# A hybrid mixer and mixture of experts on one core: GLA's decays in another PSUM bank and later, four scalings on VectorE, a longer warm-up, and part of the last expert pair's preparation one pair earlier

## The chip, the cores and the metric

The kernel runs on one core of one Trainium2 chip. The metric is the device time of one execution in microseconds (us); lower is better. PE is TensorE, DVE is VectorE, ACT is ScalarE, POOL is GpSimd, SP is SyncE, whose queue carries the weights.

## What is computed

One layer on 256 tokens of 1024 channels, all float32. A layer norm; one input projection whose columns feed an RWKV-7 group (8 heads of 64) and a GLA group (4 heads, key 64, value 128); the output projection; a residual layer norm; a top-4-of-32 mixture of experts (MoE) with a clamped SwiGLU; and a last residual layer norm. What matters here:

```python
def rwkv7_mixer(...):
    ...
    a = sigmoid(a0 + ad @ a_up)
    kk = k * k_k
    kk = kk / maximum(sqrt(sum(kk * kk, -1)), 1e-12)
    k = k * (1.0 + (a - 1.0) * k_a)
    y = rwkv7_recurrence(r, decay, k, v, kk, a)
    ...
    y = y + sum(r * k * r_k, -1) * v          # the bonus
def gla_chunked(q, k, v, gk):
    b = cumsum(gk, axis=3)                    # inside chunks of 64
    q_e = q * exp(b) * (DK ** -0.5)
    k_e = k * exp(-b)
    ...
def moe_ffn(x, ...):
    top_val, top_idx = top_k(x @ router_w + router_b, 4)
    gate = softmax(top_val)
    # for each expert e: the tokens that chose it
    h = x[tok] @ w1[e] + b1[e]
    gt = minimum(h[:, :D_FF], 7.0); up = clip(h[:, D_FF:], -7.0, 7.0)
    act = (up + 1.0) * gt * sigmoid(1.702 * gt)
    y = y.at[tok].add((act @ w2[e] + b2[e]) * gate)
x = layer_norm(x + mix); x = layer_norm(ALPHA * x + y)
```

## The kernel before

The code is written for a framework that tracks tiles and their buffers; its scheduler decides the order of the instructions on each engine from the order of the code, from priorities, and from `tc.issue_after(x)`, which keeps what is inside it behind instruction x. PSUM has eight banks of 128x512 float32: in the mixer the names p, r, s and a have two each, in the MoE g has four, x two and o two. A new `bank("p")` waits until the one before the last of that name has been read.

**The mixer, 0 to some 230 us.** The input projection is done with float32r, a shorter format that PE takes in one pass where float32 takes two (two rows of the trace for one matmul). Each weight block is cut by `split` into a high part (ACT, L382) and a low part (DVE, L385); a block of 128x512 then feeds twelve matmuls of 128x256 (L395, L396 and L397). `shift` (ACT L423, DVE L424) reads a finished projection bank and so frees it. Between the projections stand small steps of the recurrence: sums of squares (L526), a reciprocal root on ACT and DVE (its ACT part is L239), its transposes (L532) and copy (ACT, L533), its spreading over heads (L548), the scalings of k by `a` (L554, four of 128x256, on ACT), the bonus (L575), and GLA's cumulated decays (L608, four matmuls of 128x128) with their two exponentials on ACT (L610 and L611). Then come the scores of the two halves of the sequence (`scores`, L623, masked on DVE at L626), two triangular inverses on DVE (their last line is L667), the recurrence by chunks, the output projection (L992) with its norm (L994), and the router.

**The MoE, to the end.** The experts go in 16 pairs, e2 = 0 to 15, with 64 places for each expert. `places` (DVE) makes a 0/1 choice `so` of the tokens; PE gathers the chosen rows with it (L1286, from `xres`), and ACT and DVE scale the result into `xg` (L1105, L1106). For each expert of the pair W1 is applied (L1307: 8 steps of k, four matmuls each, four weight slots of 2 MB), a bias added (L1317), `swiglu` done (DVE L1084, L1086 to L1088, ACT L1085) and its result transposed (L1096). W2 follows (L1382, two slots for each expert); its result is scaled by the gate into a high and a low part (`oc`, ACT L1390, DVE L1391), and spread to the tokens by float32r matmuls with the transposed choice `soT` (L1257) in the next pair's W1, and added to `y` (L1262).

The last pair differs. Its choice times gate, `sg`, is transposed into a float32 `sgT` (L1331), and the rows of the last norm's weights are spread to all partitions (`row`, L1223, copied at L1340 into `xres`) in the middle of its W1. Its W2 goes in nine pieces of columns (L1416): each is copied by ACT into `oq` (L1418), spread by float32 matmuls (L1421), added to `y` by DVE (L1423), and, for the second expert, taken into the norm's statistics (L1425). The last norm and the stores follow.

The weights come in a list in the order of use: `fetch` issues them on SP's queue (L281), 2 MB each, into ten slots, as slots come free. Four of the list are W_out, then each pair has eight W1 slots and four W2 slots; the last pair's W2 comes in smaller pieces (`w2l`).

Of the kernel before, what the change touches and what calls it, by code (L numbers as in the profile page):

```python
# [10 lines left out]
F32 = mybir.dt.float32  # L11
# [4 lines left out]
OP = mybir.AluOpType  # L16
# [123 lines left out]
def mix_moe(ctx: ExitStack, tc: tile.TileContext, A, out, dbg=None):  # L140
# [18 lines left out]
    def bank(tag):  # L159
        return psum[0].tile([128, 512], F32, name="b" + tag, tag=tag, bufs=banks[tag])  # L160
# [12 lines left out]
    pb = bank("a")  # L173
    for _ in range(3):
        PE.matmul(pb, lhsT=wu[:, 0:128], rhs=wu, start=True, stop=True)
    nc.scalar.dma_start(cst, A["cst"][:, :ncst])
# [427 lines left out]
    enc = p1.tile([128, 2, T], F32, name="enc", tag="gs", bufs=2)  # L604
    pb = bank("p")
    for p in range(2):
        for t in range(2):
            PE.matmul(pb[:, p * T + t * 128:p * T + (t + 1) * 128], lhsT=gz[:, t, p * 128:(p + 1) * 128],  # L608
                      rhs=C("tri64"), start=True, stop=True)
    S.activation(ec.rearrange("p a t -> p (a t)"), pb, AF.Exp, scale=1.0 / 16.0)  # L610
# [653 lines left out]
    gained = [None, None]  # L1264
    pending = None
    for e2 in range(NE // 2):
        last = e2 == NE // 2 - 1
# [6 lines left out]

        so = mo.tile([128, 2, 2, 64], F32, name="so") if e2 else so0
        with tc.issue_after(placed):
            for t in range(2 if e2 else 0):
                placed = places(so, e2, t).ins
        xg = mo.tile([128, 8, 128], F32, name="xg", tag="xg")
        for ks in ((0,), (1, 2, 3), (4, 5, 6, 7)) if e2 == 0 else ((0, 1, 2, 3), (4, 5, 6, 7)):  # L1280
            pb = bank("x")
# [16 lines left out]
        for i in range(2):  # L1298
# [3 lines left out]
            for k in range(8):  # L1302
# [6 lines left out]
                if i == 0 and k == 1 and pending:  # L1309
                    scatter(*pending)  # L1310
                    pending = None
                if i == 1 and k == 4:

                    aTs.append(transposed(ups[0]))
# [4 lines left out]
            ups.append(swiglu(pg, pu))  # L1319
            if i == 0 and last:  # L1320

                sg = mo.tile([128, 2, 2, 64], F32, name="sg", tag="oc1")
                gq = gate[:, :, 2 * e2:2 * e2 + 2].unsqueeze(3).to_broadcast([128, 2, 2, 64])
                sgT = mo.tile([128, 2, T], F32, name="sgT", tag="sgT")
                pb = bank("x")
                for t in range(2):
                    V.tensor_tensor(sg[:, t], so[:, t], gq[:, t], op=OP.mult)
                for v in range(2):
                    for t in range(2):
                        for h in range(2):  # L1330
                            PE.matmul(pb[64 * h:64 * h + 64, v * T + t * 128:v * T + (t + 1) * 128], lhsT=sg[:, t, v],  # L1331
                                      rhs=ident, start=True, stop=True)
                S.activation(sgT.rearrange("p a b -> p (a b)"), pb, AF.Copy)

                ln2 = xres
                for j in range(4):
                    pb = bank("x")
                    for h in range(2):
                        row(pb[:, h * 256:(h + 1) * 256], rt, 2 * j + h)
                    S.activation(ln2[:, j // 2, j % 2 * 512:j % 2 * 512 + 512], pb, AF.Copy)  # L1340
            elif i == 0:

# [22 lines left out]
        if last:  # L1365
            aTs.append(transposed(ups[1]))
            break
# [7 lines left out]
        for i in range(2):  # L1375
            po = bank("o")
            for f in range(8):
# [26 lines left out]
    for i in range(2):  # L1404
        for j, (q, a, b) in enumerate(parts if i == 0 else parts[:3] + [(3, 0, 128), (3, 128, 256)]):
            cs = slice(q * 256 + a, q * 256 + b)
# [5 lines left out]
            with tc.issue_after(sums[-2].ins) if len(sums) > 1 else ExitStack():  # L1412
                for f in range(8):
# [81 lines left out]
```

## Time and profile before

| what | value |
|---|---|
| time, median of 3 runs | 1170.66 us (1169.7 to 1171.22) |
| the profiled execution's own time | 1169.49 us |
| its span in the trace | 1167.8 us |
| PE / PE weight loads / DVE / ACT / POOL busy | 94% / 46% / 34% / 20% / 2% of the span |
| data moved by DMA | 428.33 MB, 367 GB/s over the span |
| granted TensorE clock over the span | 0.982 of full |

The span is what the trace covers; what lies around it (1.7 us) is in the time alone. The busy shares are averages over stages with different limits, so each stage is read by itself: who waits in it, and for what. In a timeline, `[3.37 <-DVE slot L424]` says that the engine stood for 3.37 us before this row and that line 424 on DVE ended that.

### The profile page before, as it was taken

The page shows a single profiled execution, that of the slowest core. Times are in us where ns is not written, and L with a number is a line of the kernel's source. Part 1 is how long each engine was busy: PE and PEld are TensorE (multiplying, and loading weights), DVE is VectorE, ACT ScalarE, POOL GpSimd, SP SyncE. Part 2 cuts the span into 40 slices and gives each one's busy share as a digit, 9 for nine tenths or more (in the row PEclk, how much of TensorE's full clock was granted, in tenths as well). Part 3 has the DMA queues.
Part 4 walks back from the last instruction along what each step waited for, and adds up shares of the span by engine and source line. Part 5 has one row for each costly group of instructions (what it writes and reads, how often), then busy time and mean ns, then how long its engine had stood idle before and what let it go on. Part 6 is the DMA issues. An engine that isn't in the chain of part 4 may idle for free. (4 is left out here: it accounts for less than half of the span.)

```text
span 1167.8 us, 14751 instructions
## 1 busy us (share of the span) xinstructions
PE 1092.2 (94%) x6234; PEld 542.0 (46%) x6234; DVE 401.8 (34%) x849; ACT 229.6 (20%) x424; POOL 21.5 (2%) x38
## 2 busy tenths in 40 slices
PE   8989989999999999999999998899899989898995
PEld 6779976733344434343434432444333434343443
DVE  6578967403032223221222221223134223131125
ACT  5744312202120101010111110111111111111111
POOL 2000000010000000000000000000000000000001
PEclk8979999999999999999999999999999999999998
DMA  9413366589999999999999999999999999999991
GB/s 338 145 72 109 117 246 253 231 339 428 428 428 428 425 428 429 425 428 428 427 427 427 428 427 428 426 428 427 428 429 425 427 428 427 428 428 427 427 384 41
DMA packets 34988, 428.33 MB, mean 367 GB/s; under 512 B 4139, under 2 KB 4804, under 8 KB 8294
## 3 DMA queue, kind: packets, MB, share of 16 engines
q1 hardware_dynamic: 33570, 425.63, 86.9%
q10 hardware_dynamic: 1348, 1.72, 0.4%
q8 instruction: 50, 0.82, 0.3%
q14 instruction: 20, 0.16, 0.0%
HBM read 425.89 MB, written 1.05 MB: 366 GB/s over the span
## 5 line engine op out<-in xcount | busy, mean ns | idle before, releaser
L1307 PE MATMUL bg<-slot,xg 128*64 128x512 f32 x2048 | 467.9, 598 | 6.4 <-DMA slot<-w 6.4
L1307 PEld LDWEIGHTS bg<-slot,xg 128*64 128x64 f32 x2048 | 147.7, 137 | 266.1 <-issue 245.9
L1382 PE MATMUL bo<-slot,aT 128*64 128x512 f32 x960 | 220.5, 601 | 13.9 <-DMA slot<-w 11.9
L1382 PEld LDWEIGHTS bo<-slot,aT 128*64 128x64 f32 x960 | 65.9, 137 | 131.8 <-issue 109.8
L1084 DVE TENSOR_SCALAR gt<-bg 128x512 f32<-128x512 f32 x32 | 22.1, 691 | 267.5 <-PE bg L1317 267.4
L1391 DVE SCALAR_TENSOR_TENSOR oc<-bo,gp,oc 64x512 fp32r<-64x512 f32 x60 | 45.0, 750 | 160.4 <-ACT oc L1390 160.0
L1286 PEld LDWEIGHTS bx<-so,xres 128*128 128x128 f32 x512 | 66.2, 196 | 45.2 <-issue 37.2
L1286 PE MATMUL bx<-so,xres 128*128 128x128 f32 x512 | 80.2, 296 | 3.8 <-DVEq L1127 1.1
L1085 ACT ACTIVATE up<-gt 128x512 f32<-128x512 f32 x32 | 20.1, 629 | 272.2 <-DVE gt L1084 272.2
L1106 DVE TENSOR_SCALAR xg<-bx,cst 128x128 f32<-128x128 f32 x64 | 26.2, 409 | 120.8 <-PE bx L1286 108.2
L1262 DVE TENSOR_TENSOR y<-bx,y 128x512 f32<-128x512 f32 x56 | 37.3, 688 | 77.7 <-PE bx L1257 77.7
L1390 ACT ACTIVATE oc<-bo,gp 64x512 fp32r<-64x512 f32 x60 | 40.9, 682 | 103.2 <-PE bo L1382 91.6
L1257 PE MATMUL bx<-oc,soT 128*128 128x512 f32 x120 | 41.1, 446 | 9.3 <-DVE y L1262 7.0
L395 PE MATMUL bp<-xth,whi 128*128 128x256 f32 x144 | 44.7, 311 | 4.7 <-DVE slot L424 4.7
L1105 ACT ACTIVATE xg<-bx,cst 128x128 f32<-128x128 f32 x64 | 29.2, 457 | 98.1 <-PE bx L1286 97.5
L1098 ACT ACTIVATE aT<-bx 128x512 f32<-128x512 f32 x32 | 19.1, 597 | 135.1 <-PE bx L1096 135.1
L396 PE MATMUL bp<-xtl,whi 128*128 128x256 f32 x144 | 43.0, 299 | 0.0
L397 PE MATMUL bp<-xth,wlo 128*128 128x256 f32 x144 | 42.6, 298 | 0.0
L385 DVE TENSOR_TENSOR wlo<-slot,whi 128x512 fp32r<-128x512 f32 x52 | 35.5, 687 | 19.0 <-ACT whi L382 18.3
L382 ACT ACTIVATE whi<-slot 128x512 fp32r<-128x512 f32 x51 | 31.8, 629 | 45.7 <-PE bp L396 30.3
L1257 PEld LDWEIGHTS bx<-oc,soT 128*128 128x128 f32 x120 | 19.7, 194 | 40.7 <-issue 22.7
L1358 ACT ACTIVATE soT<-bx 128x256 fp32r<-128x256 f32 x30 | 11.5, 382 | 128.9 <-PE bx L1352 114.5
(424 smaller groups left out, 983.9 us busy)
## 6 DMA issues: line engine op xcount, KB each, us to landing
slot<-w SPq DMA_DIRECT2D x188, 2048.0 KB, 35.0
slot<-win SPq DMA_DIRECT2D x12, 1024.0 KB, 4.8
slot<-w2l SPq DMA_DIRECT2D x7, 1024.0 KB, 24.7
slot<-wout SPq DMA_DIRECT2D x4, 1024.0 KB, 9.1
slot<-win SPq DMA_DIRECT2D x3, 512.0 KB, 6.7
slot<-lora SPq DMA_DIRECT2D x1, 1024.0 KB, 10.7
lni<-rows SPq DMA_DIRECT2D x2, 512.0 KB, 13.7
slot<-w2l SPq DMA_DIRECT2D x2, 512.0 KB, 18.6
```

Of the source, the lines that this page charges most:

```text
L382: S.activation(hi, src, AF.Copy)
L385: (eng if b is None else (V, G)[b]).tensor_tensor(lo, src, hi.bitcast(F32), op=OP.subtract)
L395: PE.matmul(ps, lhsT=hi[:, k, :], rhs=xth[:, kk, :], start=(kk == 0), stop=False)
L396: PE.matmul(ps, lhsT=hi[:, k, :], rhs=xtl[:, kk, :], start=False, stop=False)
L397: PE.matmul(ps, lhsT=lo[:, k, :], rhs=xth[:, kk, :], start=False, stop=(kk == 7))
L1257: PE.matmul(pb, lhsT=soT[:, g, t * 128:(t + 1) * 128], rhs=ocs[g][:, h], start=(h == 0), stop=(h == 1))
L1262: V.tensor_tensor(o, pb, o, op=OP.add)
L1286: i = PE.matmul(pb[:, j * 128:(j + 1) * 128], lhsT=xres[:, t, c0:c0 + 255:2], rhs=so[:, t].rearrange("p a b -> p (a b)"), start=(t == 0), ...
L1307: PE.matmul(pp[64 * hf:64 * hf + 64, :], lhsT=lt, rhs=w[:, c0 + 512 * hf:c0 + 512 * hf + 512], start=(k == 0), stop=False)
L1382: o = PE.matmul(po[64 * half:64 * half + 64, :], lhsT=aTs[i][:, j, 64 * hf:64 * hf + 64], rhs=w[:, c0:c0 + 512], start=(f == 0), stop=(f = ...
L1390: S.activation(oc[hs, 0], po[hs], AF.Copy, scale=gp[hs, i:i + 1])
L1391: V.scalar_tensor_tensor(oc[hs, 1], po[hs], gp[hs, i:i + 1], oc[hs, 0].bitcast(F32), op0=OP.mult, op1=OP.subtract)
```

## The change

Four edits in the mixer and the warm-up, and four in the last pair. The warm-up has four and a half wide matmuls where it had three. The four scalings of k are done by DVE. GLA's four decay matmuls write a bank of the name a where they wrote one of the name p, and stand behind the bonus. In the MoE the last pair's choice and gather are made during pair 14's W1, in buffers of their own; its transposed choice (float32r now, with the gate apart as `gpL`) and the norm's rows are made during pair 14's W2. The pieces of the last pair's W2 are scaled by the gate on ACT, their remainder taken by DVE, and spread by two float32r matmuls (high and low) where one float32 matmul stood. The transposes of the last expert's SwiGLU stand behind the second piece. Lines up to L605 keep their numbers; from there on they shift (in the rows of after L608 is L609, L1286 is L1279, L1307 is L1347, L1382 is L1407, L1416 is L1446, L1421 is L1457).

```diff
-    for _ in range(3):
-        PE.matmul(pb, lhsT=wu[:, 0:128], rhs=wu, start=True, stop=True)
+    for n in (512, 512, 512, 512, 256):
+        PE.matmul(pb[:, 0:n], lhsT=wu[:, 0:128], rhs=wu[:, 0:n], start=True, stop=True)
...
-        S.activation(k2[:, p, :], ta[:, p, :], AF.Identity, scale=hka[:, p:p + 1], bias=oka[:, p:p + 1])
+        V.tensor_scalar(k2[:, p, :], ta[:, p, :], hka[:, p:p + 1], oka[:, p:p + 1], op0=OP.mult, op1=OP.add)
...
-    V.tensor_copy(bon.rearrange("p a h -> p (a h)"), pb[:, 0:16])
+    bonus = V.tensor_copy(bon.rearrange("p a h -> p (a h)"), pb[:, 0:16])
...
-    pb = bank("p")
-    for p in range(2):
-        for t in range(2):
-            PE.matmul(pb[:, p * T + t * 128:p * T + (t + 1) * 128], ...
+    pb = bank("a")
+    with tc.issue_after(bonus.ins):
+        for p in range(2):
+            for t in range(2):
+                PE.matmul(pb[:, p * T + t * 128:p * T + (t + 1) * 128], ...
...
+    so_l = mo.tile([128, 2, 2, 64], F32, name="so", tag="so1")
+    xg_l = mo.tile([128, 8, 128], F32, name="xg", tag="xg1")
+    def gather_last(ks):
...
+                PE.matmul(pb[:, j * 128:(j + 1) * 128], lhsT=xres[:, t, c0:c0 + 255:2],
+                          rhs=so_l[:, t].rearrange("p a b -> p (a b)"), start=(t == 0), stop=(t == 1))
+            gain(xg_l[:, k, :], pb[:, j * 128:(j + 1) * 128], k)
+    def choice_last():
+        for v in range(2):
+            pb = bank("x")
+            for h in range(2):
+                hs = slice(64 * h, 64 * h + 64)
+                for t in range(2):
+                    PE.matmul(pb[hs, t * 128:(t + 1) * 128], lhsT=so_l[:, t, v], rhs=ident, start=True, stop=True)
+                for t in range(2):
+                    PE.matmul(pb[hs, T + 2 * t:T + 2 * t + 2], lhsT=so_l[:, t, v], rhs=gate[:, t, 2 * NL:2 * NL + 2],
+                              start=True, stop=True)
+            S.activation(soL[:, v], pb[:, 0:T], AF.Copy)
+            V.tensor_reduce(gpL[:, v:v + 1], pb[:, T + v:T + v + 3:2], axis=AX.X, op=OP.add)
+    def ln2_rows():
...
+                if e2 == NL - 1 and i == 0 and k == 4:
+                    with tc.issue_after(placed):
+                        for t in range(2):
+                            placed = places(so_l, NL, t).ins
+                    gather_last((0, 1, 2, 3))
+                if e2 == NL - 1 and i == 1 and k == 1:
+                    gather_last((4, 5, 6, 7))
...
-            if i == 0 and last:
...
-            elif i == 0:
+            if i == 0 and not last:
...
+            if e2 == NL - 1 and i == 0:
+                choice_last()
+                ln2_rows()
...
-    oq = mo.tile([128, 4, 256], F32, name="oq", tag="oc")
+    oq = [mo.tile([128, 2, 2, 256], F32R, name="oq", tag=t_) for t_ in ("oc", "oc1")]
...
-            S.activation(oq[:, q, a:b], po, AF.Copy)
+            if i == 0 and j == 1:
+                late()
+            w = oq[q % 2][:, i]
+            S.activation(w[:, 0, a:b], po, AF.Copy, scale=gpL[:, i:i + 1])
+            V.scalar_tensor_tensor(w[:, 1, a:b], po, gpL[:, i:i + 1], w[:, 0, a:b].bitcast(F32), op0=OP.mult,
+                                   op1=OP.subtract)
...
-                o = PE.matmul(pb[:, t], lhsT=sgT[:, i, t * 128:(t + 1) * 128], rhs=oq[:, q, a:b], start=True, stop=True)
+                for h in range(2):
+                    o = PE.matmul(pb[:, t], lhsT=soL[:, i, t * 128:(t + 1) * 128], rhs=w[:, h, a:b], start=(h == 0),
+                                  stop=(h == 1))
```

How the order on PE changes, at three places. First GLA's decays: before, in the middle of the projection, right behind the sums of squares.

```order
L526 MATMUL ba<-cstm,slot 128x2 x5
L395 MATMUL bp<-xth,whi 128x256
L396 MATMUL bp<-xtl,whi 128x256
L397 MATMUL bp<-xth,wlo 128x256
L608 MATMUL bp<-cstm,slot 128x128 x4
L395 MATMUL bp<-xth,whi 128x256
L396 MATMUL bp<-xtl,whi 128x256
L397 MATMUL bp<-xth,wlo 128x256
L395 MATMUL bp<-xth,whi 128x256
```

After, at the later place where they stand now (L609), behind the bonus (L575):

```order
L397 MATMUL bp<-xth,wlo 128x256
L395 MATMUL bp<-xth,whi 128x256
L575 MATMUL ba<-cstm,slot 128x8 x8
L609 MATMUL ba<-cstm,slot 128x128 x4
L395 MATMUL bp<-xth,whi 128x256
L396 MATMUL bp<-xtl,whi 128x256
L397 MATMUL bp<-xth,wlo 128x256
L395 MATMUL bp<-xth,whi 128x256
```

The decays stood three matmuls behind the sums of squares; now 121 projection matmuls, the transposes (L532) and the spreading (L548) stand between the two. The first scores have 138 projection matmuls between them and the sums of squares, where they had 55.

Second, PE from pair 14's W2 to the last pair's W1. Before, from the end of expert 28's W2, with the last pair's gather (L1286), then its transposes (L1331) and the norm's rows (L1223) among W1:

```order
L1286 MATMUL bx<-so,xres 128x128 x8
L1382 MATMUL bo<-slot,aT 64x512 x8
L1286 MATMUL bx<-so,xres 128x128 x8
L1382 MATMUL bo<-slot,aT 64x512 x8
L1307 MATMUL bg<-slot,xg 64x512 x8
L1257 MATMUL bx<-oc,soT 128x512 x6
L1307 MATMUL bg<-slot,xg 64x512 x8
L1257 MATMUL bx<-oc,soT 128x512 x2
L1331 MATMUL bx<-cst,sg 64x128 x2
L1223 MATMUL bx<-oh,cst 128x256 x2
L1331 MATMUL bx<-cst,sg 64x128 x6
L1307 MATMUL bg<-slot,xg 64x512 x8
```

After, from the end of the transposed choice (L1290, L1292) between the two experts of pair 14's W2:

```order
L1290 MATMUL bx<-cst,so 64x128 x2
L1292 MATMUL bx<-gate,so 64x2 x2
L1407 MATMUL bo<-slot,aT 64x512 x8
L1224 MATMUL bx<-oh,cst 128x256 x4
L1407 MATMUL bo<-slot,aT 64x512 x8
L1224 MATMUL bx<-oh,cst 128x256 x4
L1347 MATMUL bg<-slot,xg 64x512 x8
L1258 MATMUL bx<-oc,soT 128x512 x4
L1347 MATMUL bg<-slot,xg 64x512 x8
L1258 MATMUL bx<-oc,soT 128x512 x4
L1347 MATMUL bg<-slot,xg 64x512 x16
```

The gather is gone from here (it stands among pair 14's W1 now, as two lots of eight); the choice and the rows stand ahead of the last pair's first W1 matmul, which has only the scatter of pair 14 between its steps.

Third, the first closing pieces. Before:

```order
L1416 MATMUL bo<-slot,aT 64x256 x8
L1096 MATMUL bx<-cst,up 128x128 x4
L1421 MATMUL bx<-oq,sgT 128x256 x2
L1416 MATMUL bo<-slot,aT 64x256 x8
L1416 MATMUL bx<-slot,aT 64x256 x8
L1421 MATMUL bx<-oq,sgT 128x256 x4
L1416 MATMUL bo<-slot,aT 64x256 x8
L1416 MATMUL bx<-slot,aT 64x256 x8
L1421 MATMUL bx<-oq,sgT 128x256 x4
```

After:

```order
L1446 MATMUL bo<-slot,aT 64x256 x8
L1457 MATMUL bx<-oq,soL 128x256
L1446 MATMUL bx<-slot,aT 64x256 x8
L1457 MATMUL bx<-oq,soL 128x256 x3
L1446 MATMUL bo<-slot,aT 64x256 x8
L1097 MATMUL bx<-cst,up 128x128 x4
L1457 MATMUL bx<-oq,soL 128x256 x8
L1446 MATMUL bo<-slot,aT 64x256 x8
```

The transposes (L1096, now L1097) moved from behind the first piece to behind the third, and where one float32 matmul spread half a piece, two float32r ones do.

## Rows read from the trace of the kernel before

**Rows 1.** The page: span, and GB/s moved in 40 equal slices.
```profile
span 1167.8 us, 14751 instructions
...
GB/s 338 145 72 109 117 246 253 231 339 428 428 428 428 425 428 429 425 428 428 427 427 427 428 427 428 426 428 427 428 429 425 427 428 427 428 428 427 427 384 41
```

**Rows 2.** Waits of SP's DMA queue: total us, times, longest.
```profile
SPq L281 <- DMA slot<-w: 448.8, 106, 5.2
...
SPq L281 <- PE bg L1307: 209.0, 54, 11.5
```

**Rows 3.** The chain of waits, last pairs: start us, us, what.
```profile
1031.84 39.10 DMA slot<-w
...
1070.98 2.79 PE bo L1382 x12
```

**Rows 4.** Windows by stage: busy per engine, PEclk, DMA share, GB/s.
```profile
60.60:83.30 22.70, 18.27 (x108) 16.68 (x107) 15.71 (x33) 9.90 (x18) 2.52 (x1) 0.70 0.21 80
...
83.30:162.80 79.50, 76.75 (x804) 70.08 (x804) 69.48 (x164) 31.19 (x54) 3.83 (x6) 1.00 0.38 147
...
1071.00:1127.90 56.90, 55.21 (x264) 22.85 (x266) 10.47 (x18) 9.20 (x16) 0.00 (x0) 0.97 1.00 425
...
1127.90:1155.00 27.10, 23.37 (x188) 15.79 (x182) 10.15 (x18) 6.15 (x14) 0.00 (x0) 1.00 0.32 132
```

**Rows 5.** PE timeline, prologue and start of the MoE.
```profile
61.06 1.05 PE L608 MATMUL bp<-cstm,slot 128*128 128x128 f32 x8
...
65.49 0.58 PE L395 MATMUL bp<-xth,whi 128*128 128x256 f32 x1 [3.37 <-DVE slot L424]
...
71.88 2.30 PE L548 MATMUL ba<-ivT,slot 8*128 8x256 f32 x8 [1.06 <-ACT ivT L533]
...
229.88 1.28 PE L1286 MATMUL bx<-so,xres 128*128 128x128 f32 x8
```

**Rows 6.** ACT timeline, 59 to 66 us.
```profile
60.19 2.08 ACT L554 ACTIVATE slot<-slot,par 128x256 f32<-128x256 f32 x4 [0.97 <-PE ba L526]
...
64.22 0.46 ACT L423 ACTIVATE slot<-bp,par 128x256 f32<-128x256 f32 x1
```

**Rows 7.** Windows of one clock level each, columns as in rows 4.
```profile
8.60:18.80 10.20, 9.57 (x38) 7.48 (x39) 8.38 (x17) 8.14 (x14) 2.33 (x8) 0.50 1.02 415
...
55.80:59.50 3.70, 3.70 (x33) 3.70 (x33) 2.51 (x6) 2.96 (x6) 0.00 (x0) 1.00 0.51 204
...
73.40:80.30 6.90, 6.90 (x33) 6.26 (x31) 6.78 (x13) 1.45 (x3) 1.59 (x1) 0.51 0.32 133
```

**Rows 8.** DVE groups by form: xcount, busy, mean ns, idle before.
```profile
L385 DVE TENSOR_TENSOR wlo<-slot,whi 128x512 fp32r<-128x512 f32 x52 | 35.5, 687 | 19.0 <-ACT whi L382 18.3 <-PE bp L404 0.2
...
L453 DVE TENSOR_SCALAR slot<-slot 128x256 f32<-128x256 f32 x1 | 0.3, 276 | 0.0
...
L994 DVE SCALAR_TENSOR_TENSOR xres<-xres,bs 128x256 f32<-128x256 f32 x2 | 0.8, 420 | 4.0 <-PE bs L992 4.0
```

**Rows 9.** PE's waits, 1041 to 1071 us.
```profile
PE bo L1382 <- DMA slot<-w: 2.0, 2, 1.1
...
PE bg L1307 <- DMA slot<-w: 1.5, 2, 1.2
```

**Rows 10.** PE groups, 1071 to 1156 us.
```profile
L1286 PE MATMUL bx<-so,xres 128*128 128x128 f32 x32 | 4.8, 294 | 0.2
...
L1421 PE MATMUL bx<-oq,sgT 128*128 128x256 f32 (+1 forms) x36 | 8.2, 367 | 1.9 <-ACT oq L1418 1.9
```

**Rows 11.** The last 2 MB weight issue, at 1081.3 us: line, then its landing.
```profile
L281 SPq DMA_DIRECT2D slot<-w x1: 328/328/328, 1081.3 to 1081.3; - x1
...
slot<-w SPq DMA_DIRECT2D x1, 2048.0 KB, 39.4
```

**Rows 12.** Timelines of the closing pieces: PE, then DVE.
```profile
1131.70 0.72 PE L1096 MATMUL bx<-cst,up 128*128 128x128 f32 x4 [1.84 <-DVE up L1088]
...
1127.95 0.69 DVE L1084 TENSOR_SCALAR gt<-bg 128x512 f32<-128x512 f32 x1 [12.60 <-PE bg L1317]
```

More of the change, by code (lines that the diff above doesn't have):

```diff
@@ L604, in mix_moe @@
     enc = p1.tile([128, 2, T], F32, name="enc", tag="gs", bufs=2)
-    pb = bank("p")
-    for p in range(2):
-        for t in range(2):
-            PE.matmul(pb[:, p * T + t * 128:p * T + (t + 1) * 128], lhsT=gz[:, t, p * 128:(p + 1) * 128],
-                      rhs=C("tri64"), start=True, stop=True)
+    pb = bank("a")
+    with tc.issue_after(bonus.ins):
+        for p in range(2):
+            for t in range(2):
+                PE.matmul(pb[:, p * T + t * 128:p * T + (t + 1) * 128], lhsT=gz[:, t, p * 128:(p + 1) * 128],
+                          rhs=C("tri64"), start=True, stop=True)
     S.activation(ec.rearrange("p a t -> p (a t)"), pb, AF.Exp, scale=1.0 / 16.0)
@@ L1265, in mix_moe @@
     pending = None
+    NL = NE // 2 - 1
+    so_l = mo.tile([128, 2, 2, 64], F32, name="so", tag="so1")
+    xg_l = mo.tile([128, 8, 128], F32, name="xg", tag="xg1")
+    soL = mo.tile([128, 2, T], F32R, name="soL")
+    gpL = mo.tile([128, 2], F32, name="gpL")
+    def gather_last(ks):
+        pb = bank("x")
+        for j, k in enumerate(ks):
+            for t in range(2):
+                c0 = k // 2 * 256 + k % 2
+                PE.matmul(pb[:, j * 128:(j + 1) * 128], lhsT=xres[:, t, c0:c0 + 255:2],
[3 more added lines that the diff above has]
+        for v in range(2):
+            pb = bank("x")
+            for h in range(2):
[8 more added lines that the diff above has]
+    def ln2_rows():
+        for j in range(4):
+            pb = bank("x")
+            for h in range(2):
+                row(pb[:, h * 256:(h + 1) * 256], rt, 2 * j + h)
+            S.activation(xres[:, j // 2, j % 2 * 512:j % 2 * 512 + 512], pb, AF.Copy)
+    ln2 = xres
     for e2 in range(NE // 2):
@@ L1273, in mix_moe @@
             overflow()
-        so = mo.tile([128, 2, 2, 64], F32, name="so") if e2 else so0
+        so = so_l if last else mo.tile([128, 2, 2, 64], F32, name="so") if e2 else so0
         with tc.issue_after(placed):
-            for t in range(2 if e2 else 0):
+            for t in range(0 if last or e2 == 0 else 2):
                 placed = places(so, e2, t).ins
-        xg = mo.tile([128, 8, 128], F32, name="xg", tag="xg")
-        for ks in ((0,), (1, 2, 3), (4, 5, 6, 7)) if e2 == 0 else ((0, 1, 2, 3), (4, 5, 6, 7)):
+        xg = xg_l if last else mo.tile([128, 8, 128], F32, name="xg", tag="xg")
+        for ks in () if last else ((0,), (1, 2, 3), (4, 5, 6, 7)) if e2 == 0 else ((0, 1, 2, 3), (4, 5, 6, 7)):
             pb = bank("x")
@@ L1311, in mix_moe @@
                     pending = None
+                if e2 == NL - 1 and i == 0 and k == 4:
+                    with tc.issue_after(placed):
+                        for t in range(2):
+                            placed = places(so_l, NL, t).ins
+                    gather_last((0, 1, 2, 3))
+                if e2 == NL - 1 and i == 1 and k == 1:
+                    gather_last((4, 5, 6, 7))
                 if i == 1 and k == 4:
@@ L1319, in mix_moe @@
             ups.append(swiglu(pg, pu))
-            if i == 0 and last:
[L1322 to L1340, printed above, removed]
-            elif i == 0:
+            if i == 0 and not last:
                 soT = mo.tile([128, 2, T], F32R, name="soT", tag="sgT")
@@ L1365, in mix_moe @@
         if last:
-            aTs.append(transposed(ups[1]))
             break
@@ L1404, in mix_moe @@
     for i in range(2):
+        if i == 0:
+            late = lambda: aTs.append(transposed(ups[1]))
         for j, (q, a, b) in enumerate(parts if i == 0 else parts[:3] + [(3, 0, 128), (3, 128, 256)]):
@@ L1417, in mix_moe @@
                               rhs=w[:, f, :], start=(f < 2), stop=(f > 5))
-            S.activation(oq[:, q, a:b], po, AF.Copy)
+            if i == 0 and j == 1:
[4 more added lines that the diff above has]
+                                   op1=OP.subtract)
             pb = bank("x")[:, 0:2 * (b - a)].rearrange("p (t c) -> p t c", t=2)
             for t in range(2):
-                o = PE.matmul(pb[:, t], lhsT=sgT[:, i, t * 128:(t + 1) * 128], rhs=oq[:, q, a:b], start=True, stop=True)
+                for h in range(2):
+                    o = PE.matmul(pb[:, t], lhsT=soL[:, i, t * 128:(t + 1) * 128], rhs=w[:, h, a:b], start=(h == 0),
+                                  stop=(h == 1))
             sums.append(o)
```

## The prediction

> **What bounds the kernel now.** I read the page first, for where the weights flow. From the tenth slice on (263 us) the GB/s line stands at 425 to 429 until the last two slices [rows 1]: the MoE is a stream of weights at one rate, and SP's queue, which issues it, waits for landings (448.8 us) far more than for any one line of PE [rows 2]. A faster engine in the middle of the MoE gains nothing. Two ends are left. The first is the moment at which the MoE starts (first gather 229.88 us [rows 5]). By then the ten slots are full, and each further transfer waits for PE to give a slot back; SP's 54 waits for L1307 [rows 2] are of that kind. So a microsecond gained ahead of 229.88 moves the whole stream by a microsecond. The second is the tail. The chain of waits is a row of landings until 1070.98, the last one of 39.10 us, and from there PE's own work [rows 3]. Between 1071.0 and 1127.9 PE is busy 55.21 of 56.90 us, and from 1127.9 to 1155.0 for 23.37 of 27.10 [rows 4]. What PE has less of behind 1070.98 counts until the stream holds it again; behind the last weight all of it counts.
>
> **The prologue.** PE's timeline around the decays shows what they cost: L608 ends near 62.1, and then PE stands 3.37 us at L395 until shift L424 has freed a bank [rows 5]. The decays had taken one of the two p banks, and the other waited for the shift's ACT part, L423, which ran at 64.22 only: ahead of it on ACT stood the four scalings (2.08 us) and a table load [rows 6]. Then PE ran at the lower of the two clock levels: 33 projection matmuls take 6.90 us at a granted clock of 0.51, where 33 at full clock take 3.70 [rows 7], 0.209 and 0.112 us each. A further 1.06 us is the wait at L548 [rows 5]. Before the first scores come 60.6 to 83.3 at a mean clock of 0.70 [rows 4].
>
> With the decays in an a bank and later, p has both banks; with the scalings on DVE, ACT reaches L423 2.08 us sooner. Upper bound, if all this goes: 3.37 + 1.06 + (6.90 - 3.70 = 3.2) for the counted slow stretch + 21 more matmuls ahead of it, between 65.5 and 70, at 0.097 saved each (2.0) = 9.6 us. In the order, 83 more projection matmuls stand ahead of the first scores; at 0.112 they are 9.3 us of PE work, the same sum from the other side. I expect the scores at about the same time (82 us) with this work done.
>
> That is a gain only where PE sets the time behind the scores. From 83.3 to 162.8 PE is busy 76.75 of 79.50, DVE 69.48 [rows 4], and the triangular inverses hang on DVE. DVE too loses work there: six of its splits' low parts (0.687 each [rows 8]) stand ahead of the scores now, 4.1 us. So the gain is at least 4.1 if DVE decides, 9.6 if PE does; nothing in these rows decides between them, and I take the middle, 6.9.
>
> Its cover: DVE gets those 4.1 and the four scalings (nearest row a TENSOR_SCALAR of the same size, 276 ns [rows 8], so 1.1) into 60.6 to 83.3, where it is busy 15.71 of 22.70 [rows 4], 7.0 free. 5.2 fit, barely; without that cover the scores come late by what does not fit, the first rival. The decays' two exponentials and their table load move behind on ACT, which is busy 9.90 of those 22.70 us and 31.19 of the next 79.50 [rows 4]: nothing. The a bank: L575's result must be copied by DVE before a further use, and what L609 overwrites was read some 22 projection matmuls before: nothing. Behind L609 in PE's row stand projections with both p banks. No DMA and nothing on SP's or POOL's queue moves here.
>
> The warm-up's added matmuls lie in time in which PE has nothing to do; what they may bring is a full clock in 8.6 to 18.8, where PE is busy 9.57 of 10.20 us at 0.50 [rows 7]. Half of 9.57 would go, but DVE is busy 8.38 there: at most 1.8, and at least nothing. I take 0.5, near the lower end, since PE still stands between the warm-up and the transposes. The Trainium skill ("TensorE: Matmul & The Clock Gate", What's actually happening) says that the clock's decision runs freely and does not restart with the kernel, so that the changeover shifts from one execution to the next; by that rule the warm-up's gain would come in some executions only, and with none the sum below is 0.5 higher. One profiled execution here can't show it.
>
> Prologue: 6.9 + 0.5 = 7.4 us.
>
> **The tail.** The gather, 4.8 us of PE [rows 10] with a wait in the middle 5.0, leaves the stretch behind 1070.98 and goes into pair 14's W1. There PE waits for landings, 2.0 + 1.5 = 3.5 us between 1041 and 1071 [rows 9], so 3.5 of the 5.0 are covered, and PE is 1.5 late at 1070.98. The choice and the norm's rows move only within the PE-bound stretch (the choice for the transposes that it replaces): nothing. PE alone would thus be ready with the last W1 at 1127.95 + 1.5 - 5.0 = 1124.45, where the first SwiGLU instruction stands at 1127.95 [rows 12]. But the last W1 slot, issued at 1081.3, lands 39.4 later [rows 11], at 1120.7, and its 16 rows and the bias follow: 56.90 / 264 rows = 0.216 each, 20 rows, 4.3. The stream allows 1125.0. I take 1125.0: 2.9 gained, with either bound within 0.6. Slots freed 1.5 late cost the stream nothing, as ten slots of 4.9 us (39.4 / 8) are 49 us against the 39.4 of a transfer.
>
> The closing, 1127.95 to the 1155.0 of the last sum, 27.1 us, has three terms. The 36 rows of float32 spreading are busy 8.2 us [rows 10]; as many float32r matmuls are 28 at 0.112 [rows 7] and 8 of half the width, 3.6 by proportion and 4.0 with an allowance for starts: 4.2 saved. PE stands 1.84 us at the transposes for SwiGLU's end [rows 12]; two more pieces stand ahead of them now: 1.8 saved. Each piece gets a DVE step between ACT's copy and the spreading. A scalar-tensor-tensor of 128x256 takes 0.42 [rows 8]. Pieces go in pairs, so four rounds pay it, 1.7, if nothing else fills PE, and nothing if it does; I take 1.7. Net 4.3. Behind 1155.0 nothing changes.
>
> Tail: 2.9 + 4.3 = 7.2 us.
>
> **Sum.** 7.4 + 7.2 = 14.6. The profiled execution, 1169.49 us with a span of 1167.8, would become 1154.9. It is 1.17 below the median of the runs, so on the median 1170.66 - 14.6 = 1156.1.
>
> **Rivals.**
> - *DVE holds the prologue.* The splits and scalings that crowd ahead of the scores make these late by as much as PE has gained, so the MoE starts when it did. For it: only 1.8 us of DVE stay free there, and DVE is in order. Against: its idle time there is spread over waits for a PE that will run faster. Time: tail alone, 1170.66 - 7.2 = 1163.5.
> - *The tail gives nothing.* The last w2 pieces arrive late for a PE that is 3 us earlier, or the new DVE step, with its reading of PSUM, costs what the matmuls save. For it: the transfers fill the stream until the last slices [rows 1], and a step of 0.42 in nine pieces is 3.8 if no two share a round. Against: DMA's share from 1127.9 to 1155.0 is 0.32 [rows 4]. Time: 1170.66 - 7.4 = 1163.3.
> - *More than that.* PE decides the prologue (9.6), the warm-up gives 1.3 and the closing steps hide (tail 9): 1150.8.
> - *No change.* The prologue's gain is lost at the inverses and the tail's at the last weights: 1170.7.
> - *Slower.* L532 and L548 hang on ACT's root and copy [rows 5] and stand in PE's row; 46 projection matmuls are queued behind L532 now. If the root comes late because DVE's part of it waits behind scalings and splits, PE stands there, the clock falls as it did behind the wait of 3.37, and all 138 matmuls run at 0.209 instead of 0.112, 13.4, plus the old stands of 4.4: 17.8 over the forecast, 1173.9. It decides from 14.6 on, which needs nearly all of these matmuls slow. Before, 54 were.
>
> **How the numbers follow.** Both parts as summed 0.58; DVE holds the prologue 0.16; the tail gives nothing 0.10; more 0.08; no change 0.04; slower 0.04. The likeliest gives 1156.1; its own range is 1152 (9.6 + 0.5 + 8.5) to 1161.6 (4.1 + 0 + 5). For 8 in 10 the range takes in the more and most of the two halves: 1150.5 to 1163.6. 0.2% is 2.3 us, about what a measurement of this kernel can tell from no change; all but the last two cases are faster by more. Faster 0.92, same 0.04, slower 0.04.
>
> **What would show it.** In the changed profile: no stand of 3 us at L395 behind the decays, and a clock near 1.0 in 60 to 83 us; the first scores near 82; the first gather (L1279 or L1280 on) near 222.5. Between 1041 and 1071 by the old count, pair 14's waits for landings gone; PE waiting for the last W1 slots; SwiGLU's first step some 2.9 nearer to the last landing of pair 15's W1; from there to the last sum near 22.8. Wrong if the scores come at 85 or later, if DVE is then busy without a gap and the second inverse ends where it did, or if pieces show PE waiting for DVE's new step for more than 0.5 us each.

## The result, and the profile after

The changed kernel took 1155.37 us (median of 4 runs, 1155.28 to 1157.1), beside 1170.18 us for the kernel before on the same chip: a ratio of 0.9887, 95% interval 0.9871 to 0.9903. That is 14.8 us less; 1156.1 was predicted, within 1150.5 to 1163.6.

The page of the changed kernel, the lines that answer to [rows 1]:

```profile
span 1153.6 us, 14794 instructions
...
GB/s 330 164 141 38 291 76 341 186 389 429 427 426 426 427 430 428 426 428 426 428 427 429 426 429 427 425 428 428 427 429 427 427 427 428 427 428 428 428 417 84
```

The stream runs at the same rate and begins earlier: the ninth slice has 389 where it had 339. The span is 14.2 us shorter. The places at which the two programs can be compared, from the first and last starts of a line's instructions (us; the last two kernels are experiments below):

| place | before | after | k2_back | decay_back |
|---|---|---|---|---|
| first projection matmul | 19.1 | 18.0 | 18.0 | 18.0 |
| first mask of the scores | 83.4 | 82.7 | 85.2 | 78.9 |
| first mask of the second half's scores | 94.1 | 85.2 | 87.7 | 89.6 |
| end of the second triangular inverse | 162.8 | 151.9 | 155.6 | 155.6 |
| first matmul with W_out | 192.7 | 184.3 | 189.3 | 188.3 |
| first gather of the MoE | 229.9 | 221.3 | 226.3 | 225.5 |
| last SwiGLU begins | 1128.0 | 1116.2 | 1120.9 | 1120.6 |
| last sum into y | 1155.1 | 1140.9 | 1145.5 | 1145.2 |

So 8.6 us came from the prologue, 3.2 from the stretch between the first gather and the last SwiGLU (898.1 before, 894.9 after), and 2.4 from the closing (27.1, now 24.7); behind the last sum nothing changed (12.7 in both).

PE's timeline in the stretch of [rows 5]. The sums of squares stand 2.3 us earlier; behind them is one stand, of 1.21 us, for a split's low part, where 3.37 and 1.06 stood. The last row is the first gather:

```profile
57.27 1.17 PE L526 MATMUL ba<-cstm,slot 128*128 128x2 f32 x10
...
61.79 0.39 PE L397 MATMUL bp<-xth,wlo 128*128 128x256 f32 x1 [1.21 <-DVE wlo L385]
...
221.26 0.40 PE L1326 MATMUL bx<-so,xres 128*128 128x128 f32 x2
```

Windows of the changed kernel, with the columns of [rows 4]. The first is the stretch in front of the scores, the second answers to the 8.6 to 18.8 of [rows 7], and the last is the closing:

```profile
57.30:82.00 24.70, 23.49 (x192) 22.46 (x192) 22.00 (x46) 12.77 (x22) 2.56 (x1) 1.00 0.35 126
8.60:18.00 9.40, 7.39 (x41) 4.90 (x42) 8.33 (x18) 7.99 (x14) 2.34 (x8) 1.00 1.02 422
...
1116.20:1141.00 24.80, 21.85 (x186) 14.59 (x182) 13.64 (x28) 6.96 (x14) 0.00 (x0) 1.00 0.47 195
```

PE runs at full clock in front of the scores (1.00; 0.70 before), and so it does behind the warm-up. DVE is busy 22.00 of 24.70 us: the cover that the prediction counted on is nearly used up.

Behind the scores, windows of the kernel before and then of the changed one, finer than [rows 4]; the last line of each is the stage from the end of the second inverse to the first matmul with W_out:

```profile
83.00:110.00 27.00, 27.00 (x206) 24.06 (x205) 22.23 (x47) 11.61 (x21) 1.22 (x4) 1.00 0.22 79
110.00:140.00 30.00, 30.00 (x294) 29.42 (x293) 27.80 (x66) 13.50 (x23) 0.00 (x0) 1.00 0.20 66
...
162.80:192.70 29.90, 26.56 (x409) 22.28 (x405) 19.41 (x49) 8.03 (x16) 0.00 (x0) 1.00 0.43 155
```

```profile
83.00:110.00 27.00, 27.00 (x219) 25.27 (x218) 24.85 (x54) 14.02 (x25) 1.22 (x4) 1.00 0.23 79
110.00:140.00 30.00, 25.39 (x332) 23.02 (x332) 28.38 (x67) 9.64 (x16) 3.28 (x2) 1.00 0.58 234
140.00:165.00 25.00, 23.99 (x371) 20.69 (x365) 16.53 (x44) 5.23 (x10) 0.00 (x0) 0.80 0.37 143
...
151.90:184.30 32.40, 31.31 (x486) 26.73 (x484) 21.12 (x53) 8.65 (x17) 0.00 (x0) 1.00 0.38 140
```

Before, PE is busy without a gap from 83 to 140: it was PE that set the time there. After, it has 4.6 us of gaps in 110 to 140 and DVE is the fuller one (28.38 of 30). Between the second inverse and W_out the changed kernel has more of both, work that moved behind the inverse: PE 31.31 us against 26.56, and DVE 21.12 against 19.41. PE fills that stage (31.31 of 32.40), which is 2.5 us longer. The clock of 0.80 in 140 to 165 is not the same in every execution, and nor is the first gather: the six profiles of kernels with this mixer have it at 220.0 (twice), 221.3, 221.5 (twice) and 221.6.

The last pair. A view of PE's waits from 1063 to 1117, which answers to [rows 9], then PE's timeline at the last W1 slot and DVE's at the last SwiGLU:

```profile
PE bg L1347 <- DMA slot<-w: 2.3, 2, 1.3
```

```profile
1112.26 3.65 PE L1347 MATMUL bg<-slot,xg 128*64 128x512 f32 x16 [1.26 <-DMA slot<-w]
```

```profile
1116.17 0.69 DVE L1085 TENSOR_SCALAR gt<-bg 128x512 f32<-128x512 f32 x1 [14.23 <-PE bg L1364]
```

Pair 14's waits for landings are gone (none from 1033 to 1063), and PE waits for the last W1 slots instead, as predicted.

One round of the closing in the chain of waits of the changed kernel (start us, us, what): two pieces, then ACT, then DVE, then the spreading.

```profile
1125.50 1.88 PE bo L1446 x16
1127.38 1.75 PE bx L1446 x16
1129.13 0.02 issue
1129.15 0.48 ACT oq L1451
1129.64 0.03 issue
1129.66 0.49 DVE oq L1452
1130.16 0.04 issue
1130.20 1.10 PE bx L1457 x7
```

From 1129.13 to 1130.20, 1.07 us, PE does one matmul (at 1129.68, with the high part); it stands 0.57 us for ACT before it and 0.13 for DVE's new step behind it. The next rounds look alike (0.57 and 0.13, then 0.47 and 0.06). In its order the piece in the x bank stands ahead of the spreading of the piece in the o bank, since they share the two x banks; both spreadings then follow together, the later piece's first.

### The profile page after: what moved, and what is told of

It reads as the page before. It is cut to its first block, busy times and chain, and to the rows that moved or that the text cites. A ratio compares the mean times of both kernels' runs of the same rounds, so it can differ in the third digit from the quotient of the medians.

```text
span 1153.6 us, 14794 instructions
## 1 busy us (share of the span) xinstructions
PE 1088.8 (94%) x6254; PEld 539.1 (47%) x6254; DVE 407.6 (35%) x862; ACT 228.2 (20%) x421; POOL 22.1 (2%) x38
## 5 line engine op out<-in xcount | busy, mean ns | idle before, releaser
L1347 PE MATMUL bg<-slot,xg 128*64 128x512 f32 x2048 | 469.3, 599 | 5.8 <-DMA slot<-w 5.8
L1347 PEld LDWEIGHTS bg<-slot,xg 128*64 128x64 f32 x2048 | 147.3, 137 | 265.1 <-issue 247.5
L1407 PE MATMUL bo<-slot,aT 128*64 128x512 f32 x960 | 218.9, 597 | 10.5 <-DMA slot<-w 8.4
L1407 PEld LDWEIGHTS bo<-slot,aT 128*64 128x64 f32 x960 | 66.2, 136 | 126.4 <-issue 104.4
L1326 PEld LDWEIGHTS bx<-so,xres 128*128 128x128 f32 x480 | 63.3, 199 | 43.3 <-issue 36.3
L1326 PE MATMUL bx<-so,xres 128*128 128x128 f32 x480 | 76.5, 300 | 3.6 <-DVEq L1128 1.1
L1099 ACT ACTIVATE aT<-bx 128x512 f32<-128x512 f32 x32 | 19.1, 597 | 129.7 <-PE bx L1097 129.7
L385 DVE TENSOR_TENSOR wlo<-slot,whi 128x512 fp32r<-128x512 f32 x52 | 37.5, 728 | 16.7 <-ACT whi L382 16.5
L395 PE MATMUL bp<-xth,whi 128*128 128x256 f32 x144 | 41.8, 291 | 1.3 <-DVE slot L424 1.3
```

The costliest lines, as they stand in the source:

```text
L385: (eng if b is None else (V, G)[b]).tensor_tensor(lo, src, hi.bitcast(F32), op=OP.subtract)
L395: PE.matmul(ps, lhsT=hi[:, k, :], rhs=xth[:, kk, :], start=(kk == 0), stop=False)
L1326: i = PE.matmul(pb[:, j * 128:(j + 1) * 128], lhsT=xres[:, t, c0:c0 + 255:2], rhs=so[:, t].rearrange("p a b -> p (a b)"), start=(t == 0), ...
L1347: PE.matmul(pp[64 * hf:64 * hf + 64, :], lhsT=lt, rhs=w[:, c0 + 512 * hf:c0 + 512 * hf + 512], start=(k == 0), stop=False)
L1407: o = PE.matmul(po[64 * half:64 * half + 64, :], lhsT=aTs[i][:, j, 64 * hf:64 * hf + 64], rhs=w[:, c0:c0 + 512], start=(f == 0), stop=(f = ...
```

## The experiments

In each, the changed kernel is the start, if nothing else is said.

**The old warm-up** (`warm_back`):

```diff
-    for n in (512, 512, 512, 512, 256):
-        PE.matmul(pb[:, 0:n], lhsT=wu[:, 0:128], rhs=wu[:, 0:n], start=True, stop=True)
+    for _ in range(3):
+        PE.matmul(pb, lhsT=wu[:, 0:128], rhs=wu, start=True, stop=True)
```

> The changed kernel with the old warm-up of three matmuls. In the changed kernel's trace PE is at full clock from 8.6 to 18 us, where it was at half before; the projection begins 1.1 us sooner and the sums of squares stand 2.3 us sooner. Theory (the 2.3 us pass through to the MoE): the sums of squares fall back to about 59.6, the first mask, the second inverse's end and the first gather come some 2 us later, 1157 to 1158. Rival (the prediction's 0.5: DVE and ACT set the scores, the 2.3 us are lost at a wait before them): the first mask moves by less than 0.7 us and the time stays within 1155 to 1156.

1157.08 us (1155.52 to 1159.08). The masks came 1.6 us later (84.3), the second inverse's end 0.3 (152.2) and the first gather 0.3 (221.5). It was run again beside the changed kernel itself (`after_again`).

> The changed kernel with the old warm-up, now against the changed kernel on the same chip. In the first profile the masks came 1.6 us later but the second inverse only 0.3, since there the clock stayed full in 140 to 165 us. Theory (the warm-up is worth 1 to 2 us, which clock falls later in the program hide in single runs): the median is 1 to 2 us above the changed kernel's. Rival (what a longer warm-up wins is absorbed before the output projection): the medians agree within 0.7.

> The changed kernel once more, beside its variants on the same chip. Its runs so far lie between 1155.3 and 1157.1 us; the same is expected, and a profile whose clock falls in 140 to 165 us (0.80 there in the first one) in some executions only, by which single runs differ by up to 2 us.

The old warm-up took 1156.98 us (1155.12 to 1160.49), the changed kernel 1157.0 (1155.36 to 1157.91). Over both calls the medians are 1156.98 of nine runs and 1155.89 of eight, 1.1 apart, with ranges of 5.4 and 2.6 us that overlap. Two of the repetition's four runs lie above the range that was expected of it. By the times the warm-up's worth is thus not settled: between nothing and some 1.5 us. The profile of the changed kernel's repetition has its masks at 84.3 and its clock at 0.83 from 75 to 85, where the first had 82.7 and 1.00; so what one program shows ahead of the scores differs by 1.6 us too:

```profile
75.00:85.00 10.00, 10.00 (x81) 9.73 (x79) 6.07 (x15) 3.63 (x5) 0.00 (x0) 0.83 0.13 40
```

That difference is the clock's. The changed kernel's two profiles and that of `gather_late` below have the same order on PE up to the first gather. In the last the clock is 1.00 in every window from 57 to 193 us, and the first gather comes at 220.0; with the fall in 140 to 165 it comes at 221.3, with the one in 75 to 85 at 221.5. The old warm-up's two profiles have it at 221.5 (full clock from 57 to 193) and at 223.0 (0.86 in 140 to 165). Where the later clock is alike, the longer warm-up thus brings the first gather 1.5 and 1.7 us forward, which speaks for the theory, though by single profiles only.

**The scalings of k back on ACT** (`k2_back`):

```diff
-        V.tensor_scalar(k2[:, p, :], ta[:, p, :], hka[:, p:p + 1], oka[:, p:p + 1], op0=OP.mult, op1=OP.add)
+        S.activation(k2[:, p, :], ta[:, p, :], AF.Identity, scale=hka[:, p:p + 1], bias=oka[:, p:p + 1])
```

> The changed kernel with the four scalings of k back on ACT. Theory (the decays' bank was the cause of the stand, and the scalings on DVE only use up a DVE that is nearly full, 22.0 of 24.7 us busy ahead of the scores): no stand of more than 1.5 us at the projection, since the second p bank covers a shift that comes 2 us late; the first mask comes up to 1.5 us sooner, 1153.9 to 1156. Rival (the scalings ahead of the shift on ACT were as much the cause): PE stands 2 to 3 us in the projection again, its clock falls behind it, 1158 to 1163.

1159.7 us (1158.99 to 1160.66), 4.3 more than in the first call and 3.8 more than the median of eight runs: in the rival's band. PE's timeline shows a stand for ACT's part of a split, which the scalings hold up:

```profile
62.10 0.39 PE L395 MATMUL bp<-xth,whi 128*128 128x256 f32 x1 [1.71 <-ACT whi L382]
```

The stand is only 0.5 longer than the 1.21 of the changed kernel, under the 2 to 3 of the rival, and no fall of the clock follows it (1.00 from 57.3 to 75). The first mask is 2.5 us later, the second inverse's end 3.7 and the first gather 5.0. My theory that a nearly full DVE would be glad of the relief fell. But most of the 5.0 does not come from this stand. Beside the repetition of the changed kernel, whose clock falls in 75 to 85 as it does here (0.83), the first mask is 0.9 later, and PE stays 0.9 behind until 134 us. There DVE's order is another one: both rows of L823 stand ahead of L689, on which PE waits, where one did. DVE in the repetition, then here:

```profile
132.58 1.16 DVE L823 TENSOR_TENSOR slot<-slot,gnw 128x512 f32<-128x512 f32 x1
133.66 0.68 DVE L689 TENSOR_TENSOR zz<-br,cstm 128x512 f32<-128x512 f32 x1
```

```profile
133.50 2.83 DVE L823 TENSOR_TENSOR slot<-slot,gnw 128x512 f32<-128x512 f32 x2
136.24 0.68 DVE L689 TENSOR_TENSOR zz<-br,cstm 128x512 f32<-128x512 f32 x1
```

The two rows take 2.83 us while POOL's L837 runs beside them (132.51 to 135.77). PE stands 2.49 us for L689 where it stood 0.82, and the clock falls behind that (0.75 in 134 to 140, 0.55 in 152 to 158; 1.00 in the repetition). So the scalings on ACT cost 0.9 us in front of the scores; the other 3.9 of 4.8 come behind another order that the scheduler made for DVE, and whether the scalings' place brings that about in general is not shown.

**The decays back in a p bank, at their old place** (`decay_back`):

```diff
-    pb = bank("a")
-    with tc.issue_after(bonus.ins):
...
+    pb = bank("p")
```

> The changed kernel with GLA's decays back in a p bank and at their old place. Theory (the bank is the cause): PE stands at the projection again behind the decays, the clock falls, fewer projection matmuls stand ahead of the first scores, and the second half's scores come late again (92 to 94 us instead of 83.5); 1160 to 1164. Rival (the shift's delay on ACT was the cause, cured by the scalings on DVE): the stand stays under 1.5 us and the time within 1 us of 1155.4.

1158.96 us (1157.07 to 1164.13), 3.6 more, or 3.1 more than the median of eight runs, and less than the theory's 1160. The ratio's interval (0.9889 to 0.9951) overlaps that of the changed kernel, so the profile has to show the loss: its first gather is 4.2 later, at 225.5, where the six profiles with the changed mixer have 220.0 to 221.6. The stand behind the decays is back, without the scalings ahead of the shift a little shorter than 3.37:

```profile
62.24 0.58 PE L395 MATMUL bp<-xth,whi 128*128 128x256 f32 x1 [2.39 <-DVE slot L424]
```

Here the first scores are earlier than in the changed kernel (first mask 78.9) and the MoE later all the same: fewer projections are done by then, and the second half's scores come at 89.6 where the changed kernel has 85.2. PE is busy for 57.0 of 57 us from 83 to 140 again, as before the change. The early scores are not what counts; the projection work done ahead of them is: 268 projection matmuls start before the first scores here and in the kernel before, 351 in the changed kernel. Both parts of the edit, the bank and the later place, are undone here at once, so which of them does it is not shown.

**The tail alone** (`tail_only`): the warm-up, the scalings and the decays as before.

> The changed kernel with all three edits of the mixer and the warm-up undone, so the tail's part alone. Theory (the two parts add): last SwiGLU some 3.1 us sooner than before, the closing 2.4 us shorter, 5.5 us in all, about 1164.7; the first gather within 0.7 us of 229.9. Rival (the tail's gain depends on the earlier start of the stream, because the last weights land at their own pace): within 2 us of 1170.2.

1163.12 us (1162.27 to 1164.66), 6.4 under the 1169.57 of the kernel before on that chip (ratio 0.9947, 0.993 to 0.9963). First gather at 230.0, last SwiGLU 895.3 behind it, closing 24.5. The tail's gain is there without an earlier start of the stream: the two parts add.

**The gather late** (`gather_late`): in the second half of pair 14's W2, with the norm's rows behind it (those lines are left out here).

```diff
-                    gather_last((0, 1, 2, 3))
-                if e2 == NL - 1 and i == 1 and k == 1:
-                    gather_last((4, 5, 6, 7))
...
+                if e2 == NL - 1 and i == 1 and f == 3:
+                    gather_last((0, 1, 2, 3))
+                    gather_last((4, 5, 6, 7))
```

> The changed kernel with the last pair's gather made in the second half of pair 14's W2 (near its old place), and the norm's rows behind it; its buffers and the early choice stay. Theory (my sum: 5.0 of gather leave a stretch in which PE never waits, 1.5 come back as lateness and the last W1 slot's landing takes up the rest): the last SwiGLU comes about 3 us later than the changed kernel's 895 us behind the first gather (1116.2 - 221.3), so 898, and the time is 1158 to 1159.5. Rival (the gather's place is worth nothing, since PE waits 1.26 us for the last W1 slot anyway): 895 to 896 and within 1 us of the changed kernel.

1157.73 us (1156.34 to 1159.9), the profiled execution being the slowest of the four. In that one the last SwiGLU comes 900.8 behind the first gather, 5.9 more than in the changed kernel. Part of this is the clock: behind the wait for a landing that is back in pair 14, it falls, as a window from 1063 to 1070 shows, and it is at 0.83 from 1090 to 1100 (the changed kernel has 1.00 in both).

```profile
1063.00:1070.00 7.00, 7.00 (x39) 3.04 (x36) 0.28 (x1) 1.28 (x2) 0.00 (x0) 0.76 1.00 424
```

Against the median of eight runs of the changed kernel (1155.89) the late gather costs 1.8 us; 3 were expected, 0 by the rival. The times alone do not tell the two kernels apart (ratio 0.9884 to 0.9921, beside 0.9871 to 0.9903); the stretch does, 900.8 where the eleven profiles with the early gather have 894.6 to 895.8. So the gather's place is worth something, and how much is not settled.

**The spread in float32** (`spread_fp32`), with `soL` and `oq` made float32 too:

```diff
-            V.scalar_tensor_tensor(w[:, 1, a:b], po, gpL[:, i:i + 1], w[:, 0, a:b].bitcast(F32), op0=OP.mult,
-                                   op1=OP.subtract)
...
-                for h in range(2):
-                    o = PE.matmul(pb[:, t], lhsT=soL[:, i, t * 128:(t + 1) * 128], rhs=w[:, h, a:b], start=(h == 0),
-                                  stop=(h == 1))
+                o = PE.matmul(pb[:, t], lhsT=soL[:, i, t * 128:(t + 1) * 128], rhs=w[:, 0, a:b], start=True, stop=True)
```

> The changed kernel with the closing spread in float32 again: one float32 copy by ACT with the gate, no remainder by DVE, one matmul of two passes for the two float32r ones. Theory (my sum: the float32r matmuls save 4.2, the DVE step costs 1.7): 2.5 us slower, about 1157.9. Rival (the DVE step stands on the path in every round and eats the saving): within 0.7 us of the changed kernel.

1156.97 us (1155.07 to 1159.17), not to be told from the changed kernel's 1157.0 in the same call: by the time, the rival. The closing, which does not depend on where the prologue ended, tells more: 25.7 us, beside 24.7 in float32r and 27.1 before. So float32r with its DVE step is worth 1.0 here, and the new order with the later transposes the other 1.4: the stand of 1.84 us is gone, and one of 0.63 for the first piece's copy is new.

**Each second piece in a g bank** (`pieces_g`):

```diff
-            po = bank("ox"[len(sums) % 2])[:, 0:b - a]
+            po = bank("og"[len(sums) % 2])[:, 0:b - a]
```

> The changed kernel with each second closing piece in a bank of the name g, which the MoE leaves free there, in place of x. In the changed kernel's order a piece in an x bank stands ahead of the spreading of the piece before it, and both spreadings follow together, the later piece's first: PE stands for ACT (0.64, 0.57, 0.57, 0.47 us) and then for DVE's new step. Theory (the shared x banks force that, so the DVE step costs its whole length in each round): with g the spreading of one piece stands behind the matmuls of the next, the stands go, and the closing falls from 24.7 to 21.5 to 22.5; 1152 to 1153.5. Rival (the stands only hide the late landing of the last weights or DVE's own load): less than 0.7 us.

1152.99 us (1151.55 to 1155.75), ratio 0.9862 (0.9841 to 0.9884), where the changed kernel in the same call has 1157.0 and 0.9896 (0.9879 to 0.9914); the two intervals overlap by little. The closing takes 22.0 us where it took 24.7, and PE is busy in all but 0.3 of it:

```profile
1117.30:1139.30 22.00, 21.70 (x186) 14.57 (x182) 13.60 (x30) 6.97 (x14) 0.00 (x0) 1.00 0.50 207
```

PE's timeline has one spreading behind each piece, without a wait:

```profile
1123.91 0.73 PE L1457 MATMUL bx<-oq,soL 128*128 128x256 f32 x4
1124.58 1.95 PE L1446 MATMUL bg<-slot,aT 128*64 128x256 f32 x16
1126.45 0.74 PE L1457 MATMUL bx<-oq,soL 128*128 128x256 f32 x4
```

**g banks and the float32 spread** (`g_fp32`), the two edits above together:

> The kernel with closing pieces in g banks and the float32 spread, so that neither has the stands at the spreadings. With the x banks the closing took 25.6 us in float32 and 24.7 in float32r, 0.9 apart. Theory (the float32r matmuls do save 4.2 of PE, and the new DVE step hid it in the stands): with g banks the closing in float32r is 22.0, and in float32 it will be 3 to 4.5 longer, 25 to 26.5. Rival (float32r is worth 1 us at most and the banks alone gave the rest): 22.5 to 23.5.

1155.68 us (1155.03 to 1157.9); the closing took 24.52 (1117.24 to 1141.76), 2.6 more than the 21.96 in float32r. Both bands were missed, the theory's by little. PE's timeline tells the size: a group of four rows in float32 goes from 1138.06 to 1139.12, 1.06 us; in float32r (above) from 1123.91 to 1124.58, 0.67. Seven such groups make 2.7. So the banks alone are worth 1.2 in float32 (25.7 to 24.5) and 2.7 in float32r (24.7 to 22.0).

```profile
1138.06 1.13 PE L1454 MATMUL bx<-oq,soL 128*128 128x256 f32 x4
1139.12 1.09 PE L1446 MATMUL bo<-slot,aT 128*64 128x128 f32 x16
```

**g banks, and the product of r and k on DVE** (`g_rk_dve`):

```diff
-    G.tensor_tensor(rk2, rT, k2, op=OP.mult)
+    V.tensor_tensor(rk2, rT, k2, op=OP.mult)
```

> The kernel with closing pieces in g banks, and the product of r and k (128x1024, 2.56 us on POOL from 68 us) done on DVE. While it runs on POOL, two DVE splits that take 0.69 each take 3.49 together. Theory (DVE's step waits for POOL's, about 2.1 us; on DVE the product takes 1.22 as the like row does): DVE wins 0.9 us ahead of the scores, the splits take 0.69 each, and the first mask comes 0 to 1 us sooner. Rival (the long split has another cause): it stays, DVE loses 1.2 us and the mask comes as much later. The time within 1.5 us of 1153 either way.

1152.47 us (1150.57 to 1152.88), ratio 0.9857 (0.9839 to 0.9875): the fastest of all, though not to be told from g banks alone. The first mask is at 82.9, beside 84.3 with g banks alone and 82.7 or 84.3 in the changed kernel, so the mask decides nothing; the rows of the splits do, and they are in the last section.

## Why the prediction was right, and where it was not

- **The bound: right.** The stream kept its rate, and its two ends gave all: 8.6 us ahead of the first gather, 5.6 behind. In every kernel here the stretch from the first gather to the last SwiGLU keeps its length (894.6 to 895.8 in the eleven profiles that have the gather in pair 14's W1), wherever the mixer ended.
- **The stand at L395 and the clock: right.** 3.37 and 1.06 became 1.21, and the clock is 1.00 in front of the scores. The scores came "at about the same time", 82.7 for 83.4.
- **DVE or PE behind the scores: the middle taken, 6.9, was low.** From the first mask to the second inverse's end the changed kernel needs 69.2 us where 79.4 stood, 10.2 less, so the upper bound, PE's, was the near one. DVE's loss of six splits there was read rightly (26 rows of L385 before, 20 after). Of the 10.2, 2.5 are given back between the inverse and W_out, where PE has 4.8 us more to do and DVE 1.7; the prediction had no term for that. The prologue gave 8.6 where 7.4 was summed. That PE was busy 57 of 57 us from 83 to 140 stood in the trace of before; a window of 79.5 us hid it.
- **The cover on DVE: thin, as said.** The first rival did not come true: 2.7 us of DVE stay free in 57.3 to 82. Undoing the decays' edit bears out that what matters is how much of the projection is done ahead of the scores: 351 matmuls against 268, the prediction's 83. Undoing the scalings' edit leaves the 351 and costs 0.9 in front of the scores; what it costs behind them comes with another order on DVE.
- **The warm-up: 0.5 taken, not settled, probably low.** From 8.6 to 18 us the clock is 1.00 in all nine profiles with the new warm-up, and 0.50, 0.64, 0.64 and 0.82 in the four with the old one. The medians differ by 1.1, and profiles that are alike later on by 1.5 and 1.7. The rule of the Trainium skill that was cited ("TensorE: Matmul & The Clock Gate", What's actually happening), by which the changeover shifts from one execution to the next, agrees with the old warm-up, where one program had 0.82 in one execution and 0.64 in the other. What the prediction made of it, a gain in some executions only, did not come: the full clock was there nine times of nine. (Without that gain the sum would be 0.5 lower, and the time 0.5 higher.)
- **The gather: 2.9 summed, 3.2 measured**, with the waits where they were predicted. The experiment bears out the sign, by the stretch in its profile, and leaves the size open.
- **The closing: 4.3 summed, 2.4 measured; the mis-sized step is the saving of the float32r matmuls.** The later transposes gave 1.4 for the 1.8 summed, and the DVE step costs about what was taken: with g banks, where PE hardly stands, float32r is 2.6 better than float32, and with x banks 1.0, so 1.6 go to the step. PE's own wait for that step, 0.13 and 0.06 us, stays under the 0.5 that the prediction named as a sign of being wrong. But 4.2 was put on the matmuls, by the 0.112 of a long row of projections, and they save 2.6; in groups of four they take 0.67, 0.167 each. And the stands themselves were not necessary: the shared x banks force them.

The sum of 14.6 for a measured 14.2 in the profiles is in part luck: the prologue gave 1.2 us more than was summed, the closing 1.9 less, and the two nearly cancel.

The slower rival (PE standing at L532 and L548 behind a late root) did not come: no stand there is in the timeline of the changed kernel.

## What to carry to other kernels

Before taking the middle between two engines' bounds, cut the stretch into windows until one of them is full without a gap; the average over a long stretch hides which sets the time. A buffer that two steps share (a PSUM bank here) can cost by the order that it forces, and the waits then name other engines (ACT and DVE here, 2.8 us in all): look which of the names is idle at that place. An edit taken back can change the scheduler's order far behind it, so see where in the trace its cost arises before putting it down to the edit. And a price from a long row of like instructions can be too low for the same instruction in short groups: 0.112 us in a row of 33 and 0.167 in groups of four here.

## What the runs showed of the hardware

DVE's split can be held up by POOL. In the repetition of the changed kernel, DVE's timeline (first fence) has two splits that take 3.49 us together while POOL's product (second fence) runs; with the product on DVE (third fence) they take 1.29.

```profile
68.29 3.49 DVE L385 TENSOR_TENSOR wlo<-slot,whi 128x512 fp32r<-128x512 f32 x2
```

```profile
68.06 2.56 POOL L568 TENSOR_TENSOR slot<-slot 128x1024 f32<-128x1024 f32 x1 [24.82 <-DVE slot L424]
```

```profile
68.38 1.22 DVE L568 TENSOR_TENSOR slot<-slot 128x1024 f32<-128x1024 f32 x1
69.51 1.29 DVE L385 TENSOR_TENSOR wlo<-slot,whi 128x512 fp32r<-128x512 f32 x2
```

So the 2.56 us on POOL cost DVE 2.2, more than the 1.22 that the work takes on DVE itself. The Trainium skill (SBUF — State Buffer, SBUF: two separate sides) says that DVE and GpSimd share a pair of ports as an exclusive lock for a whole instruction, also for a DVE instruction with two inputs in SBUF where GpSimd's own reads SBUF, and that the one that starts first has it; the trace agrees: POOL's product starts first, at 68.06, and ends at 70.62, and the first split, which takes 0.69 elsewhere, ends 0.56 behind it, at 71.18.
